# Four classical tiles first in each gated layer, evictions written ahead of the block operands, residual update and position tables issued later

## The chip, the cores and the metric

One core of one Trainium2 chip runs the whole program in one launch. The metric is device time in microseconds (us). The engines in play are TensorE (PE, matmuls; its weight loads are PEld), VectorE (DVE), ScalarE (ACT), GpSimd (POOL) and SyncE (SP), whose queue issues the weight transfers. All arithmetic is in 32-bit floats; a matmul operand is kept as a high part and a low part, so that each product takes three matmul passes.

## The reference, cut to what matters

Two networks run one after the other on one sequence of 512 tokens with 1024 features. The first is a single block (gated MLP branch, mLSTM branch, feed-forward). The second has two layers, each of them

```python
x = x + 0.5 * swiglu(rmsnorm(x, ffn1_norm), ffn1_w_gate, ffn1_w_up, ffn1_w_down)
x = x + token_mixing(rmsnorm(x, mix_norm), positions, ...)
x = x + 0.5 * swiglu(rmsnorm(x, ffn2_norm), ffn2_w_gate, ffn2_w_up, ffn2_w_down)
# swiglu(h) = (silu(h @ w_gate) * (h @ w_up)) @ w_down, 1024 -> 2816 -> 1024
```

so there are four gated layers (swiglu) in all. The change is in these four. The output of the first block is normalised by `final_g` before it becomes the residual stream `x` of the second network.

## The kernel before, in words

Activations stand with features on the 128 partitions and the 512 tokens along the free dimension, `x` as eight tiles of 128x512. `ffn` runs one gated layer. Its 2816 hidden features are 22 tiles of 128, and each tile needs a gate product and an up product over all 1024 inputs.

A tile is done in one of two ways. A *classical* tile (`Plain`) multiplies the un-normalised activations `xs` (gain folded in, split in high and low) by the gate weights and then by the up weights: 2 x 8 x 3 = 48 matmuls of 512 columns. The token factor of the rmsnorm, `norm.rb`, is applied only when the two results leave PSUM, the matmul accumulators: `t <- gate*rb` (L1043), silu on ACT (L1044), `u <- up*rb` (L1045), `t*u` (L1046), and a split of the result into `hid` (`keep`). A *block* tile (`Up`) computes gate and up together, over two halves of the inputs and of the tokens, by a scheme with seven half-size products instead of eight (`block`): 7 x 4 x 3 = 84 matmuls of 256 columns, with sums of weights (`g_block_weights`, L935 to L941 and splits) and sums of activations as operands. The last of the seven products is put off into the next item.

The activation sums come from `operands`. For each of four pairs of `x` tiles it multiplies by gain and `rb` (two L1006), forms four sums of 256 columns (`sums_of`, L895 to L899), two low parts (L900, L901) and two splits of 512 columns (`tl`). It needs `norm.rb`. In the first gated layer it also multiplies `x` itself by `final1` and by a second factor, `norm.rbx` (eight L1008).

The first three tiles of a layer are classical (`PLAIN = 3`), so that PE has work while the normalisation is finished; the other 19 are blocks. Down products (`Down`) follow from tile 5 on, and the first of them adds to `x`. Items run in a list; while item n runs, `between` steps through the weight preparation of item n+1, and raw weights are loaded three items ahead. After the last block of the first network, `norm`'s chain also issues the position tables (`g_tables`: three transfers, and operations on DVE and ACT), 10 units of planned time after `rbx`.

What sets the order: inside `ffn` only PE's instructions run in the order in which they are written. DVE, ACT, POOL and SP get their order from the compile-time scheduler, which goes by operand readiness in its own timeline and by the order of writing among what is ready. `Chain` objects such as `operands` are written when a planned clock, advanced by the matmuls, passes their next step. On each engine the resulting queue is executed strictly in order.

Buffers that matter: classical gate and up results share three PSUM banks (tag `g`), so the fourth result can only start when the first has been read; `tmp` has 7 buffers; split weights 1024 wide (`wsp`, and the two-part weight sums) have 3; raw weights 4; `slot` has 24, of which `xs` takes 8, each operand pair 3, the halves (`xhalf`) 2 and each tile's `hid` 1.

Of the kernel before, what the change touches and what calls it, by code (L numbers as in the profile page):

```python
# [15 lines left out]
ALU = mybir.AluOpType  # L16
# [7 lines left out]
KT = 8  # L24
# [74 lines left out]

CHUNKS = (5, 5, 4, 4, 4)  # L100

PLAIN = 3
H = T // 2
ORDERED = {"start": ("PE", "DVE", "Activation", "SP"), "rest": ("PE",), "gmlp": (), "heads": (), "mix": ("PE",),
           "ffn": ("PE",), "end": ("PE",)}
# [38 lines left out]
class Net:  # L144
# [612 lines left out]
    def block1_rest(self, mg):  # L757
        nc, a, x = self.nc, self.a, self.x
# [13 lines left out]
        norm = self.norm(acc)  # L772
# [61 lines left out]
        def gen():  # L834
            yield 2.5
            p0, p1 = self.tok_sum(acc[0]), self.tok_sum(acc[1])
            yield 0.6
            r = yield from self.g_rsqrt(p0, 1.0 / D, NT)
            r2 = self.tiny("r2", 4)
            nc.vector.tensor_tensor(r2, p1, r, op=ALU.mult)  # L840
            nc.vector.tensor_tensor(r2, r2, r, op=ALU.mult)
            rr = yield from self.g_rsqrt(r2, 1.0 / D, NT)
            nc.vector.tensor_tensor(rr, rr, r, op=ALU.mult)
            yield 0.4
            box.rb = yield from self.g_bcast4(rr, "rb2")
            box.rbx = yield from self.g_bcast4(r, "rbx")
            yield 10.0
            yield from self.g_tables()
        box = Chain(self, gen())
        box.rb = box.rbx = None  # L850
        box.gain = fgn
# [138 lines left out]
    def ffn(self, xs, norm, which, gain):  # L990
        nc, a, x = self.nc, self.a, self.x
        order = ExitStack()
        order.enter_context(self.in_order("ffn"))
        acts = []

        def operands():

            while norm.rb is None or which == 0 and norm.rbx is None:
                yield 0.3
            gains = norm.gain if which == 0 else self.par(("ffn1n0", "ffn2n0", "ffn1n1", "ffn2n1")[which], 0, KT)  # L1000
            half = self.halves("xhalf", 4)
            for k in range(4):
                t = [self.tmp("xr"), self.tmp("xr")]
                for i in range(2):
                    kk = k + 4 * i
                    nc.vector.scalar_tensor_tensor(t[i], x[:, kk], gains[:, kk:kk + 1], norm.rb, op0=ALU.mult, op1=ALU.mult)  # L1006
                    if which == 0:
                        nc.vector.scalar_tensor_tensor(x[:, kk], x[:, kk], self.par("final1", kk), norm.rbx, op0=ALU.mult, op1=ALU.mult)  # L1008
                acts.append(self.sums_of(*t, next(half), False))
                yield 0.5  # L1010

        operands = Chain(self, operands())
        hid = {}

        def keep(i, h):
            hid[i] = self.act_slots("hid", 1)[0]
            self.split(hid[i][0], hid[i][1], h)

        class Plain:
# [14 lines left out]
            def run(me, w, between):  # L1034
                og, ou = self.bank("g", "gate"), self.bank("g", "up")
                for n, (o, u) in enumerate(((og, w[1]), (ou, w[0]))):
                    for k, _ in enumerate(self.g_gemm(o, u, xs)):
                        if k % 3 == 2:
                            between()
                while norm.rb is None:  # L1040
                    norm.step()
                t, u = self.tmp("t"), self.tmp("u")
                nc.vector.tensor_tensor(t, og, norm.rb, op=ALU.mult)  # L1043
                nc.scalar.activation(t, t, AF.Silu)  # L1044
                nc.vector.tensor_tensor(u, ou, norm.rb, op=ALU.mult)  # L1045
                nc.vector.tensor_tensor(t, t, u, op=ALU.mult)  # L1046
                keep(me.i, t)

        class Up:

# [6 lines left out]
                return self.g_block_weights(raw)  # L1057

            def run(me, w, between):
                operands.finish()  # L1060
                t, u = self.tmp("t"), self.tmp("u")

                def on(what, o):
                    if what == "e1":
                        nc.scalar.activation(t[:, :H], o, AF.Copy)  # L1065
                    elif what == "g1":
                        nc.scalar.activation(u[:, H:], o, AF.Copy)
                    elif what == "e2":
                        nc.scalar.activation(u[:, :H], o, AF.Copy)
                    elif what == "f":  # L1070
                        nc.vector.tensor_tensor(t[:, :H], o, t[:, :H], op=ALU.add)
                        nc.scalar.activation(t[:, :H], t[:, :H], AF.Silu)
                    elif what == "g2":
                        nc.vector.tensor_tensor(u[:, :H], o, u[:, :H], op=ALU.add)
                    elif what == "e3":
                        nc.vector.tensor_tensor(u[:, H:], o, u[:, H:], op=ALU.add)
                    else:
                        nc.scalar.activation(t[:, H:], o, AF.Silu)
                        nc.vector.tensor_tensor(t, t, u, op=ALU.mult)
                        keep(me.i, t)  # L1080
                self.block(w, acts, on, between)

        nx = [None] * KT
        acc = self.acc("acc")
# [57 lines left out]
        last = len(CHUNKS) - 1  # L1142
        ups = [(Plain if i < PLAIN else Up)(i) for i in range(NF2)]
        items = []
# [11 lines left out]
        for n, item in enumerate(items):  # L1156
# [4 lines left out]
            def between():  # L1161
                if not done:
                    try:
                        next(ahead)
                    except StopIteration as e:
                        done.append(e.value)
# [5 lines left out]
        if gain:  # L1172
            norm = self.norm(acc, keep="rkeep")
# [739 lines left out]
```

## Time and profile before

| | |
|---|---|
| time before, median of 3 runs | 3039.99 us (3036.57 to 3042.76) |
| profiled execution, its own time | 3035.22 us |
| its span, first to last instruction | 3032.6 us |
| busy share of the span | PE 94%, DVE 68%, ACT 50%, POOL 14% |
| mean granted clock of TensorE | 0.978 of full |

The profile is of one execution. A busy share is a mean over stages that have different limits. The four gated layers start at about 883, 1591, 1957 and 2654 us. In the rows further down, `a <- b, c` names the tile written and the tiles read, xN is a count of instructions, and a bracket after an instruction gives the idle time of its engine before it and what ended it. Times of single instructions overlap a little on an engine: the next one starts before the previous one has written its last element.

### The profile page before, as it was taken

How to read it: one execution, taken by the hardware profiler on the slowest of the kernel's cores; microseconds unless marked ns; L12 is line 12 of the kernel's file. 1: busy time of each engine (PE TensorE's matmuls, PEld its weight loads, DVE VectorE, ACT ScalarE, POOL GpSimd, SP SyncE). 2: the span in 40 equal slices, each digit the busy share in tenths (PEclk: the TensorE clock that was granted, in tenths of full speed). 3: DMA queues.
4: the chain of work that ended last, by engine and by line, in shares of the span. 5: the costliest groups of instructions: out<-in, count | busy, mean ns of one | idle time of the engine just before them, and what ended most of it. 6: DMA issues, size and time to landing. Idle time of an engine off the chain costs nothing.

```text
span 3032.6 us, 42186 instructions
## 1 busy us (share of the span) xinstructions
PE 2865.6 (94%) x16539; PEld 2470.9 (81%) x16539; DVE 2057.9 (68%) x3350; ACT 1514.4 (50%) x2579; POOL 417.2 (14%) x255
## 2 busy tenths in 40 slices
PE   6999999999997999989998999989999899989998
PEld 5888977888876999876787999879998767879997
DVE  7665555533458676587768767686775977687675
ACT  5655444423335444477754444444444777544444
POOL 4232430000000000134410000000001344100000
PEclk9999999999998999999999999999999999999999
DMA  6334432232322323311012333323323110123332
GB/s 237 114 120 136 141 122 91 87 96 92 97 94 66 105 94 98 98 56 55 29 56 72 97 110 93 103 73 105 102 93 95 56 55 30 56 74 96 110 96 71
DMA packets 88794, 278.51 MB, mean 92 GB/s; under 512 B 9835, under 2 KB 12139, under 8 KB 88596
## 3 DMA queue, kind: packets, MB, share of 16 engines
q1 hardware_dynamic: 88596, 275.83, 28.2%
q8 instruction: 129, 2.11, 0.3%
q14 instruction: 69, 0.57, 0.1%
HBM read 273.69 MB, written 2.10 MB: 91 GB/s over the span
## 4 chain that ended last, share of the span: by engine, by line
PE 64%; DVE 13%; issue 4%; DMA 3%; ACT 3%; POOL 1%; POOLq 0%; SPq 0%; DVEq 0%; ACTq 0%
PE down L238 5%; PE down L240 5%; PE down L239 5%; PE e L238 4%; PE e L240 4%; PE ff L238 4%; PE ff L240 4%; PE ff L239 4%; PE e L239 4%; DMA wraw<-in_w2g 3%; PE g L240 2%; PE g L239 2%; PE g L238 2%; PE pv L1580 2%; PE ptr L1562 1%
## 5 line engine op out<-in xcount | busy, mean ns | idle before, releaser
L209 ACT ACTIVATE wsp<-wraw 128x1024 fp32r<-128x1024 f32 (+2 forms) x384 | 340.9, 888 | 362.8 <-issue 124.5
L210 DVE TENSOR_TENSOR wsp<-wraw,wsp 128x1024 fp32r<-128x1024 f32 (+2 forms) x318 | 320.5, 1008 | 187.3 <-ACT wsp L209 186.7
L210 POOL TENSOR_TENSOR wsp<-wraw,wsp 128x1024 fp32r<-128x1024 f32 (+1 forms) x66 | 156.3, 2371 | 946.1 <-ACT wsp L209 912.1
L240 PE MATMUL down<-hid,wsp 128*128 128x512 f32 (+1 forms) x712 | 279.3, 392 | 0.0
L238 PE MATMUL down<-hid,wsp 128*128 128x512 f32 (+1 forms) x712 | 279.1, 392 | 0.0
L239 PE MATMUL down<-hid,wsp 128*128 128x512 f32 (+1 forms) x712 | 278.7, 391 | 0.0
L209 ACT ACTIVATE a<-wraw 128x512 fp32r<-128x512 f32 x228 | 135.5, 624 | 240.5 <-DMA wraw<-in_w2g 226.1
L210 DVE TENSOR_TENSOR a<-wraw,a 128x512 fp32r<-128x512 f32 x228 | 150.9, 687 | 153.4 <-ACT a L209 153.4
L283 POOL TENSOR_TENSOR y<-ms,mhalf 128x4 f32<-128x4 f32 (+2 forms) x24 | 27.1, 1127 | 1279.7 <-DVE ms L282 1279.2
L210 DVE TENSOR_TENSOR s<-s,s 128x1024 fp32r<-128x1024 f32 x152 | 183.6, 1218 | 5.0 <-ACT s L209 5.0
L238 PE MATMUL e<-th,s 128*128 128x256 f32 x608 | 170.9, 281 | 1.3 <-ACT t L1065 1.3
L240 PE MATMUL e<-th,s 128*128 128x256 f32 x608 | 171.5, 282 | 0.0
L239 PE MATMUL e<-tl,s 128*128 128x256 f32 x608 | 170.3, 280 | 0.0
L209 ACT ACTIVATE s<-s 128x1024 fp32r<-128x1024 f32 x152 | 157.6, 1050 | 20.7 <-PE up L240 15.0
L240 PEld LDWEIGHTS down<-hid,wsp 128*128 128x128 f32 x712 | 133.8, 188 | 30.9
L239 PEld LDWEIGHTS down<-hid,wsp 128*128 128x128 f32 x712 | 133.8, 188 | 25.2
L238 PEld LDWEIGHTS down<-hid,wsp 128*128 128x128 f32 x712 | 133.9, 188 | 24.6
L1106 DVE SCALAR_TENSOR_TENSOR x<-down,x 128x512 f32<-128x512 f32 x158 | 108.3, 685 | 18.0 <-PE down L240 17.7
L238 PEld LDWEIGHTS e<-th,s 128*128 128x128 f32 x608 | 114.7, 189 | 1.5 <-ACT t L1065 1.5
L239 PEld LDWEIGHTS e<-tl,s 128*128 128x128 f32 x608 | 114.7, 189 | 0.0
L240 PEld LDWEIGHTS e<-th,s 128*128 128x128 f32 x608 | 114.4, 188 | 0.0
L437 POOL TENSOR_TENSOR ada<-ada,cb 128x1024 f32<-128x1024 f32 x32 | 86.4, 2706 | 167.6 <-DMA ada<-in_ada 162.2
(628 smaller groups left out, 8983.7 us busy)
## 6 DMA issues: line engine op xcount, KB each, us to landing
wraw<-in_w2g SPq DMA_DIRECT2D x176, 512.0 KB, 4.3
ada<-in_ada SPq DMA_DIRECT2D x48, 512.0 KB, 5.2
wraw<-in_w2d SPq DMA_DIRECT2D x96, 256.0 KB, 2.7
wraw<-in_w1f SPq DMA_DIRECT2D x44, 512.0 KB, 3.6
wraw<-in_w2d SPq DMA_DIRECT2D x64, 320.0 KB, 3.0
wraw<-in_w1a SPq DMA_DIRECT2D x32, 512.0 KB, 3.3
wraw<-in_w1b SPq DMA_DIRECT2D x32, 512.0 KB, 3.4
wraw<-in_w2f SPq DMA_DIRECT2D x28, 512.0 KB, 3.3
```

The source lines that it names most:

```text
L209: self.nc.scalar.activation(hi, src, AF.Copy)
L210: (self.nc.gpsimd if pool else self.nc.vector).tensor_tensor(lo, src, hi.bitcast(F32), op=ALU.subtract)
L238: mm(out, ah, bh, start=start, stop=False)
L239: mm(out, ah, bl, start=False, stop=False)
L240: mm(out, al, bh, start=False, stop=stop)
L283: nc.gpsimd.tensor_tensor(y, ms, self.mhalf[:, :n], op=ALU.pow)
L437: nc.gpsimd.tensor_tensor(s, s, self.cb, op=ALU.mult)
L1106: nc.vector.scalar_tensor_tensor(x[:, n], o, 0.5, x[:, n], op0=ALU.mult, op1=ALU.add)
L1562: nc.tensor.transpose(tr[:, b * P:(b + 1) * P], p[:, b * P:(b + 1) * P], self.c("ident"))
L1580: nc.tensor.matmul(o, values[b][:, h * P:(h + 1) * P], pt[i][:, b], start=b + i == 0, stop=b + i == NT)
```

## The change

`PLAIN` becomes 4, so that 18 tiles are blocks. `operands` is no longer a chain that is written when the planned clock allows: it becomes a function of one pair, and `Plain.run` writes it behind the tile's own eviction, two pairs after tile 0, one after tile 1, one after tile 2, none after tile 3 (`PAIRS`). In the first gated layer the eight multiplications of `x` are written after the first block tile instead of among the operands, and the position tables are planned 70 instead of 10 units after `rbx`. The wait for `rbx` ahead of the operands goes with it.

```diff
-PLAIN = 3
+PLAIN = 4
+
+PAIRS = ((0, 1), (2,), (3,), ())
...
-            yield 10.0
+            yield 70.0
             yield from self.g_tables()
...
-        def operands():
-
-            while norm.rb is None or which == 0 and norm.rbx is None:
-                yield 0.3
-            gains = norm.gain if which == 0 else self.par(("ffn1n0", "ffn2n0", "ffn1n1", "ffn2n1")[which], 0, KT)
-            half = self.halves("xhalf", 4)
-            for k in range(4):
-                t = [self.tmp("xr"), self.tmp("xr")]
-                for i in range(2):
-                    kk = k + 4 * i
-                    nc.vector.scalar_tensor_tensor(t[i], x[:, kk], gains[:, kk:kk + 1], norm.rb, op0=ALU.mult, op1=ALU.mult)
-                    if which == 0:
-                        nc.vector.scalar_tensor_tensor(x[:, kk], x[:, kk], self.par("final1", kk), norm.rbx, op0=ALU.mult, op1=ALU.mult)
-                acts.append(self.sums_of(*t, next(half), False))
-                yield 0.5
-
-        operands = Chain(self, operands())
+        gains = norm.gain if which == 0 else self.par(("ffn1n0", "ffn2n0", "ffn1n1", "ffn2n1")[which], 0, KT)
+        half = self.halves("xhalf", 4)
+
+        def operands(k):
+
+            t = [self.tmp("xr"), self.tmp("xr")]
+            for i, kk in enumerate((k, k + 4)):
+                nc.vector.scalar_tensor_tensor(t[i], x[:, kk], gains[:, kk:kk + 1], norm.rb, op0=ALU.mult, op1=ALU.mult)
+            acts.append(self.sums_of(*t, next(half), False))
+
...
                 keep(me.i, t)
+                for k in PAIRS[me.i]:
+                    operands(k)
...
             def run(me, w, between):
-                operands.finish()
                 t, u = self.tmp("t"), self.tmp("u")
...
                 self.block(w, acts, on, between)
+                if which == 0 and me.i == PLAIN:
+                    while norm.rbx is None:
+                        norm.step()
+                    for k in range(KT):
+                        nc.vector.scalar_tensor_tensor(x[:, k], x[:, k], self.par("final1", k), norm.rbx, op0=ALU.mult, op1=ALU.mult)
```

## Rows read from the trace of the kernel before

**Rows 1.** Waits of PE, whole span: us in total, times, longest.
```profile
PE up L238 <- DVE t L1043: 56.6, 4, 14.6
```
**Rows 2.** Timeline of PE, second gated layer: start us, duration us, instruction.
```profile
1604.09 0.39 PE L238 MATMUL gate<-xs,wsp 128*128 128x512 f32 x1
...
1624.33 0.79 PE L238 MATMUL up<-xs,wsp 128*128 128x512 f32 x1 [14.48 <-DVE t L1043]
...
1631.34 0.39 PE L238 MATMUL gate<-xs,wsp 128*128 128x512 f32 x1
...
1642.53 0.28 PE L238 MATMUL e<-bs,a 128*128 128x256 f32 x1
...
1651.04 0.28 PE L238 MATMUL e<-bs,a 128*128 128x256 f32 x1
...
1660.98 0.28 PE L238 MATMUL e<-bs,a 128*128 128x256 f32 x1
```
**Rows 3.** Timeline of ACT and DVE, second gated layer.
```profile
1602.69 0.60 ACT L319 ACTIVATE rb<-bc_b 128x512 f32<-128x512 f32 x1 [3.78 <-PE bc_b L312]
...
1604.23 1.41 DVE L1006 SCALAR_TENSOR_TENSOR xr<-x,par,rb 128x512 f32<-128x512 f32 x2
...
1618.79 1.40 DVE L1006 SCALAR_TENSOR_TENSOR xr<-x,par,rb 128x512 f32<-128x512 f32 x2
...
1623.60 0.68 DVE L1043 TENSOR_TENSOR t<-gate,rb 128x512 f32<-128x512 f32 x1
```
**Rows 4.** Busy times by stretch: us, PE, PEld, DVE, ACT, POOL, granted clock, DMA, GB/s.
```profile
1609.70:1624.30 14.60, 0.15 (x1) 0.00 (x0) 14.60 (x30) 6.54 (x11) 0.00 (x0) 0.63 0.42 141
...
1603.30:1642.50 39.20, 24.71 (x101) 19.55 (x100) 37.51 (x66) 19.62 (x31) 0.00 (x0) 0.83 0.17 54
```
**Rows 5.** Waits of PE, 880 to 960 us.
```profile
PE up L238 <- DVE t L1043: 13.1, 1, 13.1
PE bc_b L312 <- DVE ft L308: 4.3, 1, 4.3
PE e L238 <- ACT t L1065: 1.3, 1, 1.3
```
**Rows 6.** Timeline of PE and DVE, first gated layer.
```profile
900.11 0.50 PE L238 MATMUL gate<-x,wsp 128*128 128x512 f32 x1
...
904.61 0.67 DVE L1043 TENSOR_TENSOR t<-gate,rb 128x512 f32<-128x512 f32 x1
...
908.26 1.08 PE L312 MATMUL bc_b<-ft,sel 40*128 40x128 f32 x4 [4.30 <-DVE ft L308]
...
909.86 0.63 PE L239 MATMUL gate<-x,wsp 128*128 128x512 f32 x1
...
945.25 0.28 PE L238 MATMUL e<-bs,a 128*128 128x256 f32 x1
...
955.26 0.28 PE L238 MATMUL e<-bs,a 128*128 128x256 f32 x1
```
**Rows 7.** Groups of DVE, 1603.3 to 1642.5: count, busy us, mean ns.
```profile
L1006 DVE SCALAR_TENSOR_TENSOR xr<-x,par,rb 128x512 f32<-128x512 f32 x8 | 5.7, 741 | 0.0
L210 DVE TENSOR_TENSOR a<-wraw,a 128x512 fp32r<-128x512 f32 x5 | 3.3, 683 | 0.0
...
L210 DVE TENSOR_TENSOR tl<-ta,th 128x512 fp32r<-128x512 f32 x4 | 2.7, 678 | 0.0
...
L210 DVE TENSOR_TENSOR wsp<-wraw,wsp 128x1024 fp32r<-128x1024 f32 x2 | 2.4, 1216 | 0.0
...
L895 DVE TENSOR_TENSOR ta<-xr 128x256 f32<-128x256 f32 x4 | 1.7, 413 | 0.0
...
L1046 DVE TENSOR_TENSOR t<-t,u 128x512 f32<-128x512 f32 x2 | 1.4, 676 | 0.0
```
**Rows 8.** Line L1008: count, duration ns least/median/most, first and last start.
```profile
L1008 DVE SCALAR_TENSOR_TENSOR x<-x,par,rbx x8: 736/742/750, 913.0 to 934.4; 128x512 f32<-128x512 f32 x8
```
**Rows 9.** Groups of ACT, 903 to 960 us.
```profile
L1250 ACT ACT_TABLE_LOAD x2 | 2.6, 1283 | 0.0
```

## The prediction

> **What bounds the kernel now.** I read the list of PE's waits first, because PE is the busiest engine. One entry towers over the rest: the `up` matmuls of a classical tile wait four times, once in each gated layer, 56.6 us in all, for DVE's reading of a gate result [rows 1]. A difference within 0.2 percent (6 us) could not be told from no change; this wait is nine times that.
>
> Next I read the same layer on two engines, taking the second gated layer (the third and fourth share 56.6 - 14.5 - 13.1 = 29.0 us of the wait). PE starts tile 1's gate at 1604.09, finishes it some 5.6 us later and stands for 14.48 us [rows 2]. The factor `rb` is ready at 1602.69 + 0.60 = 1603.3, and tile 0's gate has long been computed, yet DVE reads it only at 1623.60, having begun the first operand pair at 1604.23 and the third at 1618.79 [rows 3]. So the first eviction stands behind three of the four pairs in DVE's queue, and with three banks for gate and up results the second `up` has nowhere to go. DVE is not idle meanwhile: it is busy for all 14.60 us of the wait, and for 37.51 of the 39.20 us from `rb` to the first block [rows 4]. That is the second thing to see: the wait is one of order, but behind it lies a stage nearly full of DVE work.
>
> In the first layer the eviction of tile 0 is early (904.61, where tile 1 began at 900.11 [rows 6]), and the same wait of 13.1 us falls on tile 2; there is one more, 4.3 us, of PE for the broadcast of `rbx` (L308 on DVE) [rows 5]. After such a wait PE runs its matmuls at 0.63 instead of 0.39 us for a while [rows 2, 6]; the granted clock in the long wait is 0.63, a mix of the two levels [rows 4].
>
> **The change part by part.** Where I count positions on PE the slow restart is included.
>
> *One more classical tile.* A classical tile takes 1642.53 - 1631.34 = 11.19 us, a block 1660.98 - 1651.04 = 9.94 us [rows 2]. This adds 1.25 us a layer, 5.0 in all.
>
> *Evictions first, second to fourth layer.* Before, PE has done three classical tiles and one whole block at 1642.53 + 9.94 = 1652.47. Afterwards, with no wait, it has done four classical tiles at 1604.09 + 3 x 11.19 = 1637.66. So at most 14.8 us are gained per layer, the extra tile paid. Tile 0's two results can be read from 1603.3 and 1604.1, in time for tile 1's `up` at 1609.7. Tile 1's gate has to be read before tile 2's `up` at about 1620.9; it is written behind two pairs (11 us), so it is due on DVE at some 1618. I cost both at nothing; if the planner lets a further pair pass, each costs up to one pair.
>
> *What is late next: DVE.* Its list from `rb` to the first block [rows 7]: a pair is two L1006 (2 x 0.741), five operations of 256 columns (5 x 0.413) and three of 512 (3 x 0.678), 5.58 us, four pairs 22.3. Three tiles' evictions are 12 operations at 0.676, 8.1. Four weight splits at 1.216 are 4.9. The first block's weights are four differences and three splits of 512 (7 x 0.68) and two splits of 1024 (2 x 1.216), 7.2. Sum 42.5, in 65 instructions. Neighbours overlap: two L1006 take 1.41, not 1.48 [rows 3], 0.072 apiece, so 37.8 us. The room to 1637.66 is 34.4. Not all of it is due then: the block's second product, 1.4 us in, needs the pairs, the evictions, the splits and some 3.6 us of the block's weights, 34.8 us in all. At the occupancy of before, 0.957 [rows 4], that takes 36.4 and is ready at 1639.7, 0.6 us late. But before, the weights of a block filled DVE's gaps from 1603 on; now those raw weights come later, as a fourth classical tile holds raw buffers, and evictions take two of the seven `tmp` buffers. At an occupancy of 0.88 it takes 39.5 and is 3.7 late. I take a new wait of 2.5 at the first block, nearer to the upper end (bounds 0 and 6). Gain 12.3 per layer, 36.9 for three.
>
> The Trainium skill, in Perfetto Trace Analysis, sections Identifying the Most-Contended Engine and Optimization Strategy, says in substance that time is won on the engine with the highest occupancy in a regime. Here that is DVE, from which the change takes nothing in these three layers. By the rule the block starts when DVE's whole list is done, 1603.3 + 37.8 = 1641.1, the gain is 11.4 a layer and the time 2.7 us above my sum; the rows say that PE's order matters more than the rule lets it.
>
> *First layer.* Before, one block is done at 955.26 plus the seventh product put off, 9.94/7 = 1.42, so 956.7. Afterwards, without waits: 900.11 + 3 x 11.19 + 1.0 for the broadcast = 934.7 [rows 6]. At most 22.0 are gained. Against it: the broadcast of `rbx` is written in tile 1, so two pairs now stand ahead of it by order of writing, where before it stood ahead of all; PE's place for it is fixed. On the other side, the block weights that filled DVE there are gone. Bounds for this wait: 0 (it fits between dependent operations) and 11 (both pairs ahead); I keep 3.0, near the measured 4.3 [rows 5]. The first block waits 2.5 as elsewhere.
>
> *Residual update and tables.* Eight L1008 at 0.742 [rows 8], 5.4 us with overlap, go from the full stage into the block stage. They are needed only by the first down product, one block later. If all eight stand ahead of a reading of a block's result, which must come within one or two products (1.4 to 2.8 us), PE could lose up to 4. The tables move by 60 planned microseconds with their DVE operations, three transfers on SP's queue ahead of later weight loads, and two table loads for Exp at 1.283 [rows 9], each with a reload for silu. Before, part of them already ran beside a block and cost PE 1.3 [rows 5]. Bounds together: gain of 1.3 and loss of 9; I take a loss of 1.5, since PE had passed this stage with only that wait. Gain of the first layer: 22.0 - 3.0 - 2.5 - 1.5 = 15.0.
>
> The Trainium skill, in ScalarE: Activation LUTs, section What ACT_TABLE_LOAD costs, prices a switch of set at about 2.66 us, a drain included, and advises batching by set. The rows show 1.283 for the load [rows 9]. At the page's price four switches would take 10.6 instead of 5.1 us of ACT, and by that estimate the sum would be some 2 us higher.
>
> *Sum.* 36.9 + 15.0 = 51.9. The profiled execution took 3035.2, so 2983.3; it lies 4.8 below the median of the runs, 3040.0, from which I forecast 2988.
>
> **The rivals.**
>
> *All cover holds.* No new waits: 3 x 14.8 + 22.0 = 66.4, 2974. For it speaks DVE's occupancy of 0.957 with any ready work; against it the list of 37.8 for a room of 34.4.
>
> *The order is not as written.* The planner takes what is ready in its own timeline. If two pairs still pass ahead of tile 0's eviction, it comes at about 1618.8, the third pair's start [rows 3], and `up` of tile 1 waits 9.8 of its 14.5 us. The gain is then 5.0 a layer and about 10 in the first, 25 in all: 3015. For it: block weights written later ran ahead of operands before. Against it: tile 0's eviction was late exactly by what was written ahead of it, and in the first layer, where it was written first, it came first, at 904.61 [rows 6].
>
> *Slower: the block starts without operands.* With four classical tiles, before `xs` is given back, 8 slots of `xs`, 12 of the pairs, 2 halves and 3 `hid` make 25 of 24. One allocation must wait for the last reading of `xs`, from about 1632.8 on (tile 3's `up`, first input). If the order makes that the third pair rather than a split of the fourth, two pairs (10.0), an eviction (2.4) and the weights (6.5), with ACT's round trips (some 3), follow it on an in-order queue: 1632.8 + 21.9 = 1654.7, 17 us after PE is ready, 2 more than the layer can gain. Four layers: 3048. It decides where the first block waits over 14.8 us. For it the count of slots; against it that the writing order puts the fourth pair last, and that only one slot is missing, for which less than 5 us of work waits.
>
> *Nothing shows.* The stage is DVE's and stays as long: the first block waits some 13 us, 3036 to 3046. The positions above speak against it.
>
> **How the numbers follow.** Forecast 2988, with its own range of 2977 to 3004: 0.72. All cover holds: 0.08. Order not as written: 0.12. Nothing shows: 0.03. Slower: 0.05. The first three are faster by over 0.2 percent, so 0.92 faster, 0.03 same, 0.05 slower. For 8 in 10 the range runs from 2973, the whole of the gain, to 3012, just short of the misplaced order.
>
> **What would show it.** In the list of PE's waits the 56.6 us entry shrinks below 10. DVE's L1043 of tile 0 follows `rb` within 2 us in all layers. PE waits for a DVE operand or weight split (`tl`, `bs`, `a`, `s`) at the first block, 1 to 4 us a layer; over 8 means that DVE is the bound. The broadcast's wait in the first layer lies between 0 and 6. Granted clock over the span rises above 0.978. The prediction is wrong if `up` still waits for L1043 for over 5 us a layer, or if the first block waits over 8.

## The result, and the profile after

The changed kernel takes 2995.78 us (median of four runs, 2988.95 to 2997.62) where the kernel before takes 3040.01 (four runs): ratio 0.9851, 95% interval 0.9832 to 0.9869, a gain of 44 us. The forecast was 2988 with a gain of 51.9. The profiled execution took 2996.43 us, its span is 2994.4, the mean granted clock 0.984 (before 0.978).

I began with the list of PE's waits after. Its columns are the waiting work, what ended the wait, us in total, times, longest.

```profile
PE e L241 <- DVE bs L902: 11.3, 4, 4.1
...
PE bc_b L314 <- DVE ft L310: 6.2, 8, 2.4
...
PE e L241 <- DVE tl L212: 5.1, 4, 1.7
...
PE e L240 <- DVE u L1072: 3.0, 4, 1.5
...
PE e L240 <- ACT bs L896: 1.7, 3, 0.6
```

The `up` entry of 56.6 [rows 1] is gone, not merely small. In its place stand three entries of the block matmuls `e` (first, third and last of the five shown), with which PE waits at the first block of each layer: 11.3 + 5.1 + 1.7 = 18.1 us. The wait for a reading of a gate result has turned into a wait for the last operand pair (`bs`) and for the low half of its split (`tl`).

The same on PE's timeline, second gated layer, the answer to [rows 2] (start, duration, instruction, idle time before it and what ended that):

```profile
1592.98 0.39 PE L240 MATMUL gate<-xs,wsp 128*128 128x512 f32 x1
...
1626.46 0.28 PE L240 MATMUL e<-bs,a 128*128 128x256 f32 x1
...
1628.28 0.38 PE L240 MATMUL e<-bs,a 128*128 128x256 f32 x1 [0.59 <-ACT bs L896]
...
1631.06 0.45 PE L241 MATMUL e<-bs,a 128*128 128x256 f32 x1 [2.39 <-DVE bs L902]
...
1637.34 0.39 PE L241 MATMUL e<-tl,s 128*128 128x256 f32 x1 [1.66 <-DVE tl L212]
...
1641.94 0.28 PE L240 MATMUL e<-bs,a 128*128 128x256 f32 x1
```

Tile 1 starts at 1592.98 and the first block at 1626.46: three classical tiles at 11.16 us each, with no gap. But that block lasts 15.5 us, to 1641.94, where a block whose operands are there lasts 8.5 (in the experiment with two pairs behind tile 1, below, the second layer's goes from 1636.83 to 1645.33). So 7.0 us are lost: 4.64 in waits, and most of the rest because PE runs slower behind the second of them, one matmul of 256 columns every 0.21 us (starts at 1631.52, 1631.73, 1631.94) instead of every 0.12 (1626.46, 1626.59, 1626.70); the granted clock is 0.50 there for 3.4 us (last section), which is 1.7 us.

DVE in the same stretch, for [rows 3, 4]. First the timeline, then two windows (length, busy time of PE, its weight loads, DVE, ACT, POOL with counts, granted clock, DMA share, GB/s):

```profile
1592.21 0.69 DVE L1038 TENSOR_TENSOR t<-gate,rb 128x512 f32<-128x512 f32 x1 [2.65 <-ACT rb L321]
...
1621.37 0.68 DVE L212 TENSOR_TENSOR a<-wraw,a 128x512 fp32r<-128x512 f32 x1
...
1624.83 0.69 DVE L937 TENSOR_TENSOR s<-wraw 128x512 f32<-128x512 f32 x1
...
1628.44 0.69 DVE L938 TENSOR_TENSOR s<-wraw 128x512 f32<-128x512 f32 x1
...
1630.58 0.42 DVE L902 TENSOR_TENSOR bs<-xr,bs 128x256 fp32r<-128x256 f32 x1
...
1636.60 0.69 DVE L212 TENSOR_TENSOR tl<-tb,th 128x512 fp32r<-128x512 f32 x1
1637.20 0.69 DVE L212 TENSOR_TENSOR hid<-t,hid 128x512 fp32r<-128x512 f32 x1
1640.56 0.69 DVE L937 TENSOR_TENSOR s<-wraw 128x512 f32<-128x512 f32 x1 [2.67 <-DMA wraw<-in_w2g]
```

```profile
1592.20:1637.90 45.70, 41.06 (x187) 33.84 (x186) 45.40 (x77) 25.11 (x41) 0.00 (x0) 0.96 0.24 74
```

```profile
1592.20:1626.50 34.30, 34.30 (x150) 27.69 (x149) 34.01 (x57) 19.15 (x29) 0.00 (x0) 1.00 0.26 81
```

Tile 0's gate is read the moment `rb` is there. From then on DVE has almost no hole: 45.40 us busy of 45.70, and the pairs' last result (`tl`, 1636.60) stands at the end of that window. In it stand operations of the *next* block (the `a`, L937 and L938 shown from 1621.37 to 1628.44, ahead of the last L902), and right behind it DVE is idle for 2.67 us.

From tile 0's gate to the start of tile 6, which is a block in every kernel here (its first `e`), is called a layer's *stretch* below. The stretches go from 102.1 to 88.9 us in the first layer, 88.2 to 82.0, 89.1 to 80.7 and 88.6 to 80.3: 13.3 + 6.2 + 8.4 + 8.3 = 36.2 us of the 38.2 by which the two spans differ. The second layer gained less because its second block waits 1.5 us for an eviction (the entry `DVE u L1072` above) and takes 20.1 us where the third and fourth layer's takes 18.3. The rest of the 38.2 lies between the stretches: the two long parts, of 605 and 607 us before, became 2.1 longer and 3.8 shorter, and over all the builds below they lie between 603 and 611. So a difference of a few us between two builds' times need not come from the gated layers, and the stretches are read beside them.

### The profile page after: what moved, and what is told of

It reads as the page before. It is cut to its first block, busy times and chain, and to the rows that moved or that the text cites. A ratio compares the mean times of both kernels' runs of the same rounds, so it can differ in the third digit from the quotient of the medians.

```text
span 2994.4 us, 41860 instructions
## 1 busy us (share of the span) xinstructions
PE 2872.5 (96%) x16395; PEld 2469.8 (82%) x16395; DVE 2040.7 (68%) x3318; ACT 1500.0 (50%) x2549; POOL 416.4 (14%) x255
## 4 chain that ended last, share of the span: by engine, by line
PE 69%; DVE 11%; issue 3%; ACT 2%; DMA 1%; POOL 1%; SPq 0%; POOLq 0%; DVEq 0%; ACTq 0%
PE down L242 5%; PE down L241 5%; PE down L240 5%; PE e L241 4%; PE e L240 4%; PE e L242 4%; PE ff L240 4%; PE ff L242 4%; PE ff L241 4%; PE g L242 2%; PE g L241 2%; PE g L240 2%; PE pv L1581 2%; PE ptr L1563 2%; PE wo L242 1%
## 5 line engine op out<-in xcount | busy, mean ns | idle before, releaser
L211 ACT ACTIVATE wsp<-wraw 128x1024 fp32r<-128x1024 f32 (+2 forms) x392 | 349.7, 893 | 392.6 <-issue 133.5
L212 DVE TENSOR_TENSOR wsp<-wraw,wsp 128x1024 fp32r<-128x1024 f32 (+2 forms) x326 | 334.6, 1027 | 187.1 <-ACT wsp L211 186.2
L211 ACT ACTIVATE a<-wraw 128x512 fp32r<-128x512 f32 x216 | 127.8, 623 | 227.1 <-DMA wraw<-in_w2g 218.4
L212 DVE TENSOR_TENSOR a<-wraw,a 128x512 fp32r<-128x512 f32 x216 | 142.6, 685 | 142.9 <-ACT a L211 142.9
L212 DVE TENSOR_TENSOR s<-s,s 128x1024 fp32r<-128x1024 f32 x144 | 173.6, 1217 | 2.3 <-ACT s L211 2.2
L241 PE MATMUL e<-tl,s 128*128 128x256 f32 x576 | 163.4, 284 | 5.1 <-DVE tl L212 5.1
L242 PE MATMUL e<-th,s 128*128 128x256 f32 x576 | 162.4, 282 | 0.0
L240 PE MATMUL e<-th,s 128*128 128x256 f32 x576 | 162.2, 282 | 0.0
L211 ACT ACTIVATE s<-s 128x1024 fp32r<-128x1024 f32 x144 | 149.3, 1051 | 9.3 <-DVE s L943 3.1
L1107 DVE SCALAR_TENSOR_TENSOR x<-down,x 128x512 f32<-128x512 f32 x158 | 108.2, 685 | 18.1 <-PE down L242 17.7
L240 PEld LDWEIGHTS e<-th,s 128*128 128x128 f32 x576 | 109.9, 191 | 0.0
L242 PEld LDWEIGHTS e<-th,s 128*128 128x128 f32 x576 | 109.0, 189 | 0.0
```

The source lines that it names most:

```text
L211: self.nc.scalar.activation(hi, src, AF.Copy)
L212: (self.nc.gpsimd if pool else self.nc.vector).tensor_tensor(lo, src, hi.bitcast(F32), op=ALU.subtract)
L240: mm(out, ah, bh, start=start, stop=False)
L241: mm(out, ah, bl, start=False, stop=False)
L242: mm(out, al, bh, start=False, stop=stop)
L1107: nc.vector.scalar_tensor_tensor(x[:, n], o, 0.5, x[:, n], op0=ALU.mult, op1=ALU.add)
```

## The experiments

Theory D: the stage up to the first block is full of DVE work, and each us of it that must pass before the last operand pair is paid by PE. Theory O: it is still a question of order on DVE. The two theories part where the amount is changed without the order, and the other way round. Each run stands beside runs of the kernel before on the same chip; ratios are to these.

**Order alone (three classical tiles, with the later update and tables).**

```diff
-PLAIN = 4
-PAIRS = ((0, 1), (2,), (3,), ())
+PLAIN = 3
+PAIRS = ((0, 1), (2,), (3,))
```

> Order part alone: three classical tiles, evictions ahead of the operand pairs, the rest as in the changed kernel. Theory D (the first block waits because DVE's list of work after rb is longer than PE's room): without the fourth tile the room shrinks by 11.2 us and the list only by 2.7 + 2.4 (an eviction and two weight splits), so the first block waits some 5 us longer than the 7.0 us lost there in the changed kernel, about 12 to 13 a layer; the up wait is gone (16.1 a layer). Gain over the kernel before some 4 a layer, 10 in the first: about 3018. Rival O (the wait comes from work of the next block being queued ahead of the last pair, an error of order): the same 7.0 us are lost, gain 9 a layer: about 3003 or less.

3034.6 us, ratio 0.998 (0.9964 to 0.9997). Both theories missed: nearly nothing is left of the gain.

```profile
PE e L240 <- ACT bs L896: 23.4, 4, 7.1
...
PE up L240 <- DVE t L1038: 13.8, 3, 4.7
...
PE e L241 <- DVE bs L902: 8.4, 4, 3.6
```

The wait only moved: 13.8 us of it stay at `up`, and 31.8 went to the operands of the first block, which comes a tile earlier here and finds DVE's list further from its end. The second layer's stretch is 88.4 us, as before (88.2).

**The fourth tile alone (kernel before, `PLAIN = 4`).**

> Fourth classical tile alone in the kernel before: operands as a chain, written ahead of the evictions, residual update and tables where they were. Theory: the up wait of 13 to 14.6 us a layer stays, and each layer pays 1.25 us for the tile; the first block does not wait, as before. 3040 + 5 = 3045. Rival (the fourth tile itself removes part of the wait, as it gives DVE room): below 3030.

3026.7 us, 0.9958 (0.9944 to 0.9971), which is the rival's side:

```profile
PE up L238 <- DVE t L1043: 46.1, 4, 14.1
```

`up` waits 46.1 us instead of 56.6, and the first block does not wait for operands; in the second layer the wait is 10.64 us. The parts alone are worth 4 and 12 us against 44 together: the order takes away the wait ahead of the pairs, and the fourth tile gives PE work while the pairs are made. Each helps little without the other.

**Less DVE work, by GpSimd: the second pair's sums and splits.**

```diff
-            acts.append(self.sums_of(*t, next(half), False))
+            acts.append(self.sums_of(*t, next(half), k == 1))
```

> Changed kernel with the sums and splits of the second operand pair on GpSimd instead of DVE (four operations of 256 columns and two of 512, 2.6 us of DVE a layer). Theory D (DVE's amount of work): the first block waits 2.6 us less and the slow restart after it shrinks too, 3 to 4 us a layer: about 2982. Rival O (order or latency of the pairs): GpSimd's pair takes 5 us or more, nothing is gained or it is late itself: 2994 to 3005.

2999.3 us, 0.987 (0.9842 to 0.9898), no faster than the change and within the rival's range. In the second layer, GpSimd, then DVE, then PE:

```profile
1599.94 4.07 POOL L897 TENSOR_TENSOR ta<-xr 128x256 f32<-128x256 f32 x1 [13.89 <-DVE hid L212]
```

```profile
1607.75 1.21 DVE L1005 SCALAR_TENSOR_TENSOR xr<-x,par,rb 128x512 f32<-128x512 f32 x1 [1.89 <-POOL tl L212]
```

```profile
1617.28 0.50 PE L242 MATMUL gate<-xs,wsp 128*128 128x512 f32 x1 [1.75 <-DVE wsp L212]
```

The first operation on GpSimd, on 256 columns, took 4.07 us, where DVE takes 0.42. DVE's next pair then waited 1.89 us for GpSimd's split, and PE 1.75 us for a weight split ahead of the first block, which still lost 4.8 us.

**Less DVE work, by GpSimd: weight splits of the third and fourth tile**, which are due only a tile later.

```diff
-                    out.append(self.split_weights(r, KT, P))
+                    out.append(self.split_weights(r, KT, P, pool=me.i > 1))
```

> The changed kernel, with the weight splits of the third and fourth classical tile on GpSimd instead of DVE: in each layer four operations of 1024 columns fewer on DVE, 4.9 us, before the first block. Unlike the second pair, whose sums come out of a chain of dependent operations, these weights are known one tile ahead. Theory D (amount): the first block's loss of 7 falls to about 2 a layer, some 5 x 4 = 20 us less, 2974 to 2980, and no wait of over 1 us for a split. Rival (GpSimd is too slow, as with the pair): the gate or up of tile 2 or 3 waits for its split, 3 us and more a layer, 2996 to 3010.

3007.3 us, 0.9907 (0.9881 to 0.9933), the rival's time, and the rival's wait is there: PE's gate matmuls wait for GpSimd's splits, in the second layer 2.8 us at tile 2 and 1.1 at tile 3.

```profile
PE gate L242 <- POOL wsp L212: 11.7, 6, 2.8
```

There is a second cause that no theory had. GpSimd's first three splits, then DVE beside them, second layer:

```profile
1595.19 2.48 POOL L212 TENSOR_TENSOR wsp<-wraw,wsp 128x1024 fp32r<-128x1024 f32 x1 [7.87 <-ACT wsp L211]
1602.19 8.96 POOL L212 TENSOR_TENSOR wsp<-wraw,wsp 128x1024 fp32r<-128x1024 f32 x2 [4.53 <-ACT wsp L211]
```

```profile
1594.66 3.56 DVE L1005 SCALAR_TENSOR_TENSOR xr<-x,par,rb 128x512 f32<-128x512 f32 x2
...
1606.69 2.23 DVE L212 TENSOR_TENSOR tl<-ta,th 128x512 fp32r<-128x512 f32 x1
1608.85 2.59 DVE L901 TENSOR_TENSOR tb<-xr,tb 128x256 f32<-128x256 f32 x1
1611.36 0.68 DVE L1040 TENSOR_TENSOR u<-up,rb 128x512 f32<-128x512 f32 x1
```

While the four splits run, four DVE rows that read two SBUF tiles are stretched by 1.6 to 2.2 us: L901 takes 2.59 us instead of 0.42, two L1005 3.56 instead of 1.40. Together they add 2.16 + 1.55 + 2.17 + 1.59 (an L903 of 2.27 instead of 0.68) = 7.5 us to DVE, more than the 4 x 1.22 = 4.9 taken off. So this says nothing against D: it did not make DVE's list shorter, and it made PE late ahead of the first block. The time lost is mostly in the first layer, whose stretch is 94.8 us instead of 88.9; the second's is 81.9, as in the changed kernel. The Trainium skill, GPSIMD Engine Reference, section Specifications, says that GpSimd shares its way into SBUF with the vector engine and contends with DVE instructions of two SBUF inputs; this trace agrees so far as every stretched one is of that kind and the two L1038 inside those spans, with one operand in PSUM, keep 0.68. Others with two SBUF inputs keep their time as well, so it is not each of them.

**One more room for the same work: five classical tiles.**

```diff
-PLAIN = 4
-PAIRS = ((0, 1), (2,), (3,), ())
+PLAIN = 5
+PAIRS = ((0, 1), (2,), (3,), (), ())
```

> Changed kernel with five classical tiles first (pairs after tiles 0, 0, 1, 2). Theory D: DVE gets 11.2 us more room for 2.7 + 2.4 us more work, the first block's loss of 7 us goes, the tile costs 1.25: 2996 - 4 x 5.7 = about 2973. Rival S (slots: 26 are wanted of 24 before xs is given back, so the last pair or an eviction waits for xs whatever the room): the loss stays and the tile is paid, about 3001.

2978.8 us, 0.9792 (0.9756 to 0.9827). That is D's direction, if not all of its 2973: the waits at the first block are gone altogether, and the second layer's stretch falls from 82.0 to 74.5 us although the extra tile costs PE 1.25. The rival, a wait for slots that stays whatever the room, is out.

**The order pinned: the next block's weights behind the last pair.**

```diff
-                return self.g_block_weights(raw)
+                g = self.g_block_weights(raw)
+                while True:
+                    with self.tc.issue_after(self.pair_done.ins) if me.i == PLAIN + 1 else ExitStack():
...
+                            next(g)
...
+                    yield
```

> The changed kernel (2996), with DVE's work on the first block's successor (its a, weight differences and splits) held behind the last operand pair. Theory D (DVE is full in the stage, so the first block's wait of about 7 us a layer is a question of the amount of its work): the work of 2.4 us that ran ahead only changes place, the first block starts 2.4 earlier and the next one waits for its weights instead; 2994 to 3000, block 4 to block 6 as long as before (about 25 us). Theory O (the wait is one of order, as the wait removed was): DVE has 2.7 us of idle time after the pairs into which this work fits, the first block's wait shrinks by 2.4 a layer and part of the slow restart goes with it, 10 to 14 us in all, 2982 to 2987.

2981.5 us, 0.982 (0.9789 to 0.985); the kernel with the update held, which ran beside it, took 2995.6. That is theory O, with a gain of 14 us between the two. PE in the second layer:

```profile
1622.98 0.28 PE L240 MATMUL e<-bs,a 128*128 128x256 f32 x1
...
1625.17 0.39 PE L241 MATMUL e<-bs,a 128*128 128x256 f32 x1 [0.84 <-DVE bs L902]
...
1627.31 0.39 PE L241 MATMUL g<-tl,s 128*128 128x256 f32 x1 [0.45 <-DVE tl L212]
...
1633.31 0.28 PE L240 MATMUL e<-bs,a 128*128 128x256 f32 x1
```

The block lasts 10.3 us instead of 15.5, and the stretch 76.1 instead of 82.0; the block behind it takes 19.3, 1.0 more than the 18.3 of the other layers in the changed kernel. So D as I stated it was too strong: DVE is full, but 5.3 us of what it did in the changed kernel before the last `tl` was not due then (of the next block's weights, seven operations at 0.60 from start to start and a split at 1.14), and part of it fits into DVE's idle time behind the pairs.

**Two pairs behind tile 1 instead of one.**

```diff
-PAIRS = ((0, 1), (2,), (3,), ())
+PAIRS = ((0, 1), (2, 3), (), ())
```

> The changed kernel, with two pairs behind tile 0 and two behind tile 1 instead of two, one, one. Theory D: the amount is the same and DVE is full, so the wait only moves: the eviction of tile 2's gate comes one pair (5.6 us) later and tile 3's up waits for it by about 4 us a layer, the first block by 3 less; 2994 to 3004. Theory O (only the place of the last pair counts): the pair ends a tile earlier, the first block's loss falls to about 2, no other wait; 2976 to 2982.

3005.9 us, 0.9904 (0.9878 to 0.9929): D's direction, and more than it expected. There is no wait at the first block, and `up` of tile 3 waits again:

```profile
PE up L240 <- DVE t L1038: 29.7, 4, 8.5
```

**The residual updates really out of the stage.** The change writes them behind the first block, but in its trace they run as ready work between dependent operations: six start by 926.34, the last two at 938.56 and 939.56, around the start of that block (939.09), and all eight stand ahead of the last pair's L902.

```profile
909.86 2.73 DVE L1082 SCALAR_TENSOR_TENSOR x<-x,par,rbx 128x512 f32<-128x512 f32 x4
...
938.56 0.74 DVE L1082 SCALAR_TENSOR_TENSOR x<-x,par,rbx 128x512 f32<-128x512 f32 x1
...
939.56 0.74 DVE L1082 SCALAR_TENSOR_TENSOR x<-x,par,rbx 128x512 f32<-128x512 f32 x1
...
944.10 0.41 DVE L902 TENSOR_TENSOR bs<-xr,bs 128x256 fp32r<-128x256 f32 x1
```

```diff
-                    for k in range(KT):
-                        nc.vector.scalar_tensor_tensor(x[:, k], ...)
+                    with self.tc.issue_after(me.e3.ins):
+                        for k in range(KT):
+                            nc.vector.scalar_tensor_tensor(x[:, k], ...)
```

> The changed kernel, with the eight residual updates of the first gated layer held behind the first block's last reading, so that they really leave the classical stage (in the changed kernel six of them ran in it as fillers). Theory D: 6 x 0.67 = 4.0 us less DVE work ahead of the first block; in the first layer the first block's loss falls from 6.7 to 2 to 3 us, the other layers stay, 2991 to 2993, to be read from the positions rather than from the time. Rival: the updates filled gaps of DVE only and cost nothing, the loss stays at 6 to 7 and the block after waits longer; 2996 to 3000.

2995.6 us, 0.9872 (0.9847 to 0.9897), no change in the time. In the first layer the first block lasts 11.1 us instead of 15.2, about D's size, but the next one 19.9 instead of 18.3, since the updates now stand ahead of its evictions. Tile 1 also lasts 17.7 us instead of 16.2 behind the same wait of 2.4 for the broadcast, at a granted clock of 0.81 instead of 0.89. The stretch is 1.3 us shorter in all.

**Updates and tables written early again** (updates behind tile 2's pair, tables 10 units after `rbx`).

```diff
-            yield 70.0
+            yield 10.0
...
+                if which == 0 and me.i == 2:
+                    for k in range(KT):
+                        nc.vector.scalar_tensor_tensor(x[:, k], ...)
```

> The changed kernel with one part undone: in the first gated layer the eight residual updates are written behind tile 2's pair (ahead of the first block) and the position tables are planned 10 units after rbx again. The second to fourth layer stay as they are. Theory D (in this stage every DVE operation ahead of the first block is paid by PE): six of the eight updates ran there anyway, so 2 x 0.67 us of them and the tables' operations are added, the first layer from tile 0 to block 6 grows from 88.9 by 3 to 6 us; 2999 to 3002. Rival (moving them was worth nothing, they fill gaps wherever they are written): 88 to 90 us, 2994 to 2998.

3011.1 us, 0.9897 (0.988 to 0.9913); the first layer's stretch grows from 88.9 to 97.4 us, more than D expected. Two of PE's waits in the first layer, then DVE's reading of tile 2's gate in the changed kernel and here:

```profile
938.48 0.80 PE L240 MATMUL up<-x,wsp 128*128 128x512 f32 x1 [6.00 <-DVE t L1038]
...
953.55 0.58 PE L241 MATMUL e<-tl,s 128*128 128x256 f32 x1 [3.15 <-DVE tl L212]
```

```profile
930.89 0.41 DVE L900 TENSOR_TENSOR tb<-xr,ta 128x256 f32<-128x256 f32 x1
931.22 0.67 DVE L1038 TENSOR_TENSOR t<-gate,rb 128x512 f32<-128x512 f32 x1
```

```profile
929.23 0.41 DVE L900 TENSOR_TENSOR tb<-xr,ta 128x256 f32<-128x256 f32 x1
...
932.31 0.51 DVE L1225 TENSOR_SCALAR posc<-posj 128x4 f32<-128x4 int32 x6
...
937.74 0.68 DVE L1038 TENSOR_TENSOR t<-gate,rb 128x512 f32<-128x512 f32 x1
```

In the changed kernel tile 2's gate is read right behind L900; here 8.2 us of other work stand between, 2.0 of them table operations (L1223 to L1250) and the rest operand and weight work of the blocks. So tile 3's `up` waits as `up` did before the change. No update is among that work: the same six run ahead of it in both kernels. Why the scheduler put weight work there too is not shown. Of the 8.5 us, 1.5 are tile 1 at a lower clock, as in the experiment before. The profiled execution took 3004.7, 8.2 above the change's, and this layer accounts for that. The other three runs lie near 3011; what they add has no trace here.

**Both holds on four tiles.**

```diff
+                    with self.tc.issue_after(self.pair_done.ins) if me.i == PLAIN + 1 else ExitStack():
...
+                    with self.tc.issue_after(me.e3.ins):
```

> Four classical tiles with both holds: the next block's weights behind the last operand pair (2981 alone) and the residual updates behind the first block's last reading (1.3 us of the first layer alone). If both act on the same wait, the first layer loses 2 us at the first block instead of 4.9, and the time is 2978 to 2981, about that of five tiles (2979). Rival: the updates then delay the evictions of the block after as they did alone, and it stays at 2981 to 2984.

2987.7 us, 0.982 (0.9805 to 0.9835): the rival's mechanism, and by ratio no better than the weights' hold alone (0.982), which ran on another chip. The two holds meet in the first layer: eight updates (six of them shown) stand ahead of the next block's weight split, and PE waits for it.

```profile
949.75 4.06 DVE L1091 SCALAR_TENSOR_TENSOR x<-x,par,rbx 128x512 f32<-128x512 f32 x6
953.73 2.35 DVE L212 TENSOR_TENSOR s<-s,s 128x1024 fp32r<-128x1024 f32 x2
```

```profile
955.00 0.58 PE L242 MATMUL g<-th,s 128*128 128x256 f32 x1 [5.91 <-DVE s L212]
```

**The update held on five tiles.**

```diff
+PLAIN = 5
+PAIRS = ((0, 1), (2,), (3,), (), ())
...
+                    with self.tc.issue_after(me.e3.ins):
```

> Five classical tiles (2979, no wait at the first block) with the residual updates held behind the first block's last reading. Theory D: DVE's amount no longer decides once the room is a tile longer, so nothing is gained, 2977 to 2981. Rival (the updates still cost as fillers): first layer 2 to 4 us shorter, 2974 to 2977.

2974.8 us (2974.27 to 2976.32), 0.9783 (0.9769 to 0.9797). This is the fastest of all, below the change's interval; whether the hold adds anything to five tiles isn't told apart, as the intervals overlap and the first layer is 0.8 us shorter (82.9 against 83.7).

## Why the prediction came out as it did

**The wait removed: right.** The entry vanished, tile 0's gate is read at once, and from the second layer on PE passes the classical tiles without a gap: in the second, 1592.98 to 1626.46 is 3 x 11.16, where I had 3 x 11.19. The fourth tile's price and the cap of 14.8 us a layer stand.

**The new wait at the first block: the right place, the wrong size. This is the step that failed.** I took 2.5 us, with 6 as the bound; it cost 7.0, 7.0 and 6.9 us in the second to fourth layer and 6.7 in the first. The waits alone are 4.6 to 4.7 us a layer, above the 1 to 4 that I had named as the sign and below the 8 that would have made the prediction wrong. Three things were wrong in its working:

- The list was too short. The 37.8 us held evictions of three tiles; the fourth's has no place that keeps it behind the pairs, and ran among them: 4 x 0.60 = 2.4.
- I expected holes, an occupancy of 0.88 to 0.957. There were almost none (0.993), but they had been filled by work of the next block, seven operations and a split: 7 x 0.60 + 1.14 = 5.3. With both, 37.8 + 2.4 + 5.3 = 45.5, against 45.4 busy in the window. I had treated the filler of before as a help (it leaves less to do later); on an engine without holes each filler is in front of something.
- I priced the wait itself only. 4.64 us of waiting cost 7.0: 1.7 more is the lower clock, and the last 0.7 lies in the starts around the waits.

The form of the sum held. With the two missing parts, the 34.8 us that I had called due become 42.5, and at 0.993 they would be ready 7.1 us late; that this is so near the 7.0 lost is in part luck, as the lower clock is not in it.

Cap less loss, 14.8 - 7.0 = 7.8, is about what the layers gained (6.2, 8.4, 8.3; 12.3 was forecast), the second with the 1.8 us of its second block against it. Over four layers the step is 4.5 + 4.5 + 4.4 + 4.2 = 17.6 us too small. The gain forecast missed what the layers gave by 51.9 - 36.2 = 15.7: the first layer's other terms came out 2.5 better than forecast, and the later layers 0.6 worse.

**First layer: near, by errors that partly cancel.** 13.3 for 15.0. The broadcast waits 2.42 us (3.0 taken, 4.3 before [rows 5]). The first block lost 6.7 instead of 2.5. The 1.5 us for the residual update and the tables did not show: from block 5 to block 6 it is 18.25 us, as in the third and fourth layer (18.3). Nor were the updates really moved: all eight stayed ahead of the last pair. What the writing places did bring is seen by undoing them: 8.5 us of the first layer, 1.5 of them by the clock, and the rest where table operations and weight work stood ahead of tile 2's gate.

**The sentences on the Trainium skill.** By the rule of the Trainium skill's Perfetto Trace Analysis, sections Identifying the Most-Contended Engine and Optimization Strategy, as the prediction applied it, a block starts when DVE's whole list is done, and the sum was to come out 2.7 us higher. The trace puts the truth between: DVE is the engine almost without a hole, as the rule has it, but with the list as it was (45.5 us from 1592.2) the block would start at 1637.7, 11.2 us late, and it lost 7.0, since PE did part of the block meanwhile. The rule's figure fell short for the same reason as mine, the list. For the switch of tables, the kernel with the tables written early shows five loads of 1.28 us in the stage. Around the one at 950.25 ACT loses no further time, as the activation before ends at 950.24 and the next starts at 951.54; PE's two large waits there end with DVE.

**The rivals.** "All cover holds" fell by 18.1 us of new waits. "The order is not as written" fell with the first eviction, though a part of it is true of the residual updates. "Nothing shows" is what the order does without the fourth tile. No wait for a slot of `xs` was seen.

**The level.** The profiled execution before lay 4.8 us below its median, the one after 0.6 above its own. So the spans show 38 us and the medians 44; against its own profile the forecast missed by 13 us, against the median by 8. That the medians come out nearer to the forecast than the profiles do is luck.

## What to carry to other kernels

When a stage is full on one in-order engine, make the list of all that the scheduler can put there, not of what is due: a ready operation goes ahead of something, and here a later writing place did not move the eight updates out of the stage. Taking away a wait by order was worth little until the waiting engine also got other work for the time that the list takes; here order gave 4 us, the extra tile 12, both 44, and a second extra tile some 17 more. A filler held back explicitly was worth nearly as much as that tile, where the engine had idle time behind the hold, and the hold on the updates, whose work met evictions instead, was worth nothing in the time.

## What the runs showed of the hardware

GpSimd beside DVE: one split of 1024 columns takes 2.43 us where DVE is not in its way (mean of 58 in the kernel after) and 4.04 beside the full stage (mean of four, second layer, third and fourth tile's splits moved). A DVE instruction with two SBUF inputs that meets it takes up to 2.2 us longer. In 15 of the 16 splits moved, exactly one such instruction is stretched, and it ends 0.55 us (512 columns) or 0.28 us (256) after the split does; in the rows shown, the split ends at 1597.67 and the two L1005 at 1598.22. So moving an elementwise operation to GpSimd cost DVE more than doing it, 7.5 us for 4.9.

A short wait on PE can cost more than itself. Behind waits of 0.59 and 2.39 us in the second layer's first block, the granted clock is 0.50 for 3.4 us, the lower of the levels 1.2 and 2.4 GHz, where it was 1.00 in the 34 us ahead; behind the third wait, of 1.66 us, it stayed at 1.00. The block, then the slow part of it:

```profile
1626.50:1642.00 15.50, 10.86 (x74) 10.25 (x73) 12.84 (x23) 7.91 (x14) 0.00 (x0) 0.89 0.22 69
```

```profile
1631.25:1634.65 3.40, 3.40 (x17) 3.40 (x17) 3.40 (x7) 2.71 (x5) 0.00 (x0) 0.50 0.03 5
```

It need not: with the second pair on GpSimd, waits of 1.61, 0.71 and 1.67 us in the same block left the clock at 1.00. There 3.99 us of waiting cost 4.8, here 4.64 cost 7.0.

```profile
1628.00:1641.40 13.40, 9.41 (x75) 8.75 (x74) 12.80 (x23) 6.76 (x12) 0.00 (x0) 1.00 0.23 79
```
